# Attention kernel: one scan for a block's first piece, value rows added 1024 wide, and the operands of projection A made while the last gate runs

## The chip, the cores and the metric

The kernel runs on one core of one Trainium2 chip. Its engines work in parallel, each in the order of its own queue: PE (TensorE, matrix products; the profile lists its weight loads apart, as PEld), DVE (VectorE), ACT (ScalarE), POOL (GpSimd) and SP, which issues the DMAs. The metric is the time of one execution in microseconds of the device, lower is better. Before the change the median of three runs is 1477.73 us (1476.61 to 1478.14).

## The reference, cut to what matters

One layer of an encoder: 1024 positions, width 1024. Branch A is softmax attention over a band of nine chunks with a learned bias, branch B is stick-breaking attention; each has 8 heads of 64. The branches are projected, gated, added, projected once more, and followed by a norm, a gated feed-forward and a second norm.

```python
h = x @ w_in
y_a = chunk_band_attention(qa, ka, va, rel_bias) @ w_proj_a
y_b = stick_breaking_attention(qb, kb, vb) @ w_proj_b
mix = (sigmoid(ga + b_a) * y_a + sigmoid(gb + b_b) * y_b) @ w_out
x = layer_norm(alpha * x + mix)
x = layer_norm(alpha * x + (silu(g) * u) @ w_ffn_out)      # g, u = split(x @ w_ffn_in)

# branch B, for every query t and key s < t:
#   weight[t, s] = sigmoid(z[t, s]) * product over s < j < t of sigmoid(-z[t, j])
```

## The kernel before, in words

All products are in fp32 made of three passes of rounded operands: `split` (lines 106 and 107) rounds a tile on ACT and subtracts on DVE, so a tile `x` becomes `xh` and `xl`. The stages, by the profiled execution's clock: projections of the input (to 289 us), attention (289 to 688), projection B and output projection (688 to 860), feed-forward in (860 to 1259) and feed-forward out (1259 to the end).

In attention the 16 heads (8 of A, then 8 of B) run one behind the other. The rows of the sequence are reversed, so key positions run forward from the diagonal. A head has eight query blocks of 128; the first four make row group g = 0 and the last four g = 1. For a block, PE computes scores into a PSUM bank (`sc`, two banks). In A (`soft_block`) DVE adds the bias and takes the running minimum (line 494, listed as ISA in the order of instructions), ACT takes the exponential (499), DVE a reciprocal (501), POOL multiplies (502). In B (`stick_block`) ACT makes sigmoid(-z) in `kp` and sigmoid(z) in `be`; DVE turns `kp` into running products by scans along the row; POOL multiplies `be` by them (537). A block of B wider than 512 is cut into two pieces. Its first 128 columns hold the diagonal: there the scan multiplies and adds the identity, which starts the product at 1; further on nothing is to be added. `ident_ps` is a PSUM bank that holds the identity in its first 128 columns and zeros behind.

`value_steps` then transposes weights on PE (558, tile `tp`), splits them (tile `pt`), and multiplies by the values into one PSUM bank (`pv`, 571 and 572), two steps behind the transposes. At the end of a row group ACT copies `pv` out (578), and DVE adds its lower 64 rows to its upper 64 rows (579). Two heads make one tile `yt` of 128x1024, which is stored to `y_dr` (581); the last tile, number 7, stays in SBUF.

Between these steps PE is filled with the units of `fill_all`: first gates 4 to 15 (48 matmuls each, line 420), then projection A (608), whose operands `yh` and `yl` come from `y_dr` through `reload_y` (load on SP, rounding on ACT at 632, subtraction on POOL at 633). `yh` and `yl` take the buffers (tag `xt`) that hold the gates' operand. A scheduler in the framework sets the order of each engine's queue from the written order and its own model of times, and buffers come in rings (`SLOTS`), so an edit in one place can move rows elsewhere.

After attention, projection B works on tiles c = 6, 7, 5, 4, 0, 1, 2, 3, two halves each: 12 matmuls into a `sc` bank, then on DVE a product with the gate `gB` (736), a sum with A's part (737) and a subtraction (107), with ACT's rounding `mh` between. SP loads `gB`, and the output weights `wr_o` into a ring of three buffers; each `wr_o` is rounded on ACT (403) and subtracted on DVE (404, `wl_o`).

Of the kernel before, what the change touches and what calls it, by code (L numbers as in the profile page):

```python
# [14 lines left out]
ALU = mybir.AluOpType  # L15
# [3 lines left out]
P = 128  # L19
# [3 lines left out]
DH = 64  # L23
# [10 lines left out]
LO, HI = slice(0, HW), slice(HW, 2 * HW)  # L34
# [14 lines left out]
def hybrid_trunk_kernel(ctx: ExitStack, tc, x, xt, w_in, b_gate, rel_bias, w_proj,  # L49
# [6 lines left out]
    nc = tc.nc  # L56
# [7 lines left out]
    def slot(tag, name, dtype=F32):  # L64
        return pool.tile([P, 1024], dtype, tag=tag, name=name, bufs=SLOTS[tag])
# [10 lines left out]
    def bank(tag, name):  # L76
        return ps.tile([P, HW], F32, tag=tag, name=name, bufs=BANKS[tag])

    def dram(name, n):
        return [dr.tile([P, 1024], F32, name=f"{name}{i}") for i in range(n)]  # L80
# [3 lines left out]
    dma = nc.sync.dma_start  # L84
# [12 lines left out]
    y_dr = dram("y_dr", 8)  # L97
# [7 lines left out]
    def split(dst_h, dst_l, src):  # L105
        nc.scalar.copy(dst_h, src)  # L106
        nc.vector.tensor_tensor(dst_l, src, dst_h.bitcast(F32), ALU.subtract)  # L107
# [302 lines left out]
    def load_gate(i, lo_eng):  # L410
        return load_w(w_in[24 + (i % 2) * 8 + i // 2], f"g{i}", of("op"), of("op"), lo_eng)

    def gate(i, w):
        gt = slot("gt", f"gate{i}")
        for hf, cs in enumerate((LO, HI)):
            acc = bank("mm", f"gps{i}_{hf}")
            for k in range(KT):
                ks = slice(k * P, (k + 1) * P)
                for j, (lw, rx) in enumerate(((w[0], xh), (w[0], xl), (w[1], xh))):
                    mm(acc, lw[:, ks], rx[k][:, cs], start=(k == j == 0),  # L420
                       stop=(k == KT - 1 and j == 2))
                    yield 1.0
            nc.scalar.copy(gt[:, cs], acc)
        dma(g_dr[i], gt)
# [34 lines left out]
    def scores(name, hd, b, c0, n):  # L459
        q = hd["qs"][:, b * P:(b + 1) * P]  # L460
        ksl = slice(b * P + c0, b * P + c0 + n)
        sc = bank("sc", name)
        mm(sc[:, 0:n], q, hd["kh"][:, ksl], start=True, stop=False)
        mm(sc[:, 0:n], q, hd["kl"][:, ksl], start=False, stop=True)  # L464
        return sc
# [40 lines left out]
    def ident_ps():  # L506


        if not aside:
            aside.append(bank("tr", "ident_ps"))  # L510
            nc.vector.memset(aside[0], 0.0)
            nc.vector.tensor_copy(aside[0][:, 0:P], ident)
        return aside[0]

    def stick_block(hd, b, be):

        nm = f"b{hd['n']}_{b}"
        w = (8 - b) * P
        kp = slot("kp", f"kp_{nm}")
        nc.gpsimd.memset(be[:, 0:1], 0.0)  # L520
        c1 = max((4 - b) * P, 320)
        cuts = [(0, c1), (c1, w - c1)] if b < 4 else [(0, w)]
        for c0, n in cuts:
            sc = scores(f"sc_{nm}_{c0}", hd, b, c0, n)
            e = c0 + n
            m0 = max(c0, 1)
            nc.scalar.activation(kp[:, c0:e], sc[:, 0:n], AF.Sigmoid, scale=-1.0)  # L527
            nc.scalar.activation(be[:, m0:e], sc[:, m0 - c0:n], AF.Sigmoid)
            if c0 == 0:

                nc.vector.tensor_tensor_scan(kp[:, 0:P], kp[:, 0:P], ident_ps()[:, 0:P], 0.0,
                                             ALU.mult, ALU.add)
            s0 = max(c0, P)
            if s0 < e:
                nc.vector.tensor_tensor_scan(kp[:, s0:e], kp[:, s0:e], ident_ps()[:, 0:e - s0],  # L535
                                             kp[:, s0 - 1:s0], ALU.mult, ALU.bypass)
            nc.gpsimd.tensor_tensor(be[:, m0:e], be[:, m0:e], kp[:, m0 - 1:e - 1], ALU.mult)  # L537

    def value_steps(hd, g, wt):

        br, h = hd["br"], hd["h"]
        reach = (4, 8)[br]
        q0 = 4 * g
        nm = f"{'ab'[br]}{hd['n']}_{g}"
        pv = []

        kbs = [4, 5, 6, 7, 3, 2, 1, 0] if g == 0 else [7, 6, 5, 4]
        steps = []
        for i, kb in enumerate(kbs):
            lo_q = max(q0, kb - reach)  # L550
            hi_q = min(q0 + 3, kb)
            n = (hi_q - lo_q + 1) * P
            pts = []

            def turn(kb=kb, lo_q=lo_q, hi_q=hi_q, n=n, pts=pts):
                tp = bank("tr", f"tp_{nm}_{kb}")
                for qb in range(lo_q, hi_q + 1):
                    tr(tp[:, (qb - lo_q) * P:(qb - lo_q + 1) * P],  # L558
                       wt[qb - q0][:, (kb - qb) * P:(kb - qb + 1) * P], ident)
                pt = slot("pt", f"pt_{nm}_{kb}", F32R)  # L560
                split(pt[:, 0:n], pt[:, HW:HW + n], tp[:, 0:n])
                pts.append(pt)

            def mult(i=i, kb=kb, lo_q=lo_q, n=n, pts=pts):
                v = hd["v"]
                if i == 0:
                    pv.append(bank("pv", f"pv_{nm}"))
                last = i == len(kbs) - 1
                cs = slice((lo_q - q0) * P, (lo_q - q0) * P + n)
                pt = pts[0]  # L570
                mm(pv[0][:, cs], v[:, kb, :], pt[:, 0:n], start=(i == 0), stop=False)
                mm(pv[0][:, cs], v[:, kb, :], pt[:, HW:HW + n], start=False, stop=last)
                if last:
                    yt = hd["yt"]()
                    r = slice(h * DH, (h + 1) * DH)
                    gs = slice(g * HW, (g + 1) * HW)
                    both, cs = (yt, gs) if h == 0 else (slot("yt", f"yv_{nm}"), LO)
                    nc.scalar.copy(both[:, cs], pv[0])
                    nc.vector.tensor_tensor(yt[r, gs], both[0:DH, cs], both[DH:P, cs], ALU.add)
                    if h == 1 and g == 1 and hd["i"] < 7:  # L580
                        dma(y_dr[hd["i"]], yt)

            steps.append((turn, mult, i == 0))
        return steps


    def fill_all():
        w = first_w
        for i in range(first_gate, 16):
            nxt = load_gate(i + 1, nc.gpsimd) if i < 15 else load_proj(0, 0, "op", nc.gpsimd)  # L590
            yield from gate(i, w)
            w = nxt
        for i in range(4):
            reload_y(i, nc.gpsimd)
        for cc in range(4):
            nxt = load_proj(0, cc + 1, "op", nc.gpsimd) if cc < 3 else None
            if cc < 3:
                reload_y(4 + cc, nc.gpsimd)
            for j in range(2):
                c = 2 * cc + j  # L600
                t = slot("gt", f"gA{c}")
                reload_gate(t, c, 0)
                for hf, cs in enumerate((LO, HI)):
                    acc = bank("mm", f"yAps{c}_{hf}")
                    for k in range(4):
                        ks = slice(j * HW + k * P, j * HW + (k + 1) * P)
                        for n, (lw, rx) in enumerate(((w[0], yh), (w[0], yl), (w[1], yh))):
                            mm(acc, lw[:, ks], rx[k][:, cs], start=(k == n == 0),  # L608
                               stop=(k == 3 and n == 2))
                            yield 1.0  # L610
                    nc.vector.tensor_tensor(t[:, cs], acc, t[:, cs], ALU.mult)
                if c < KEEP:
                    dma(m_dr[c], t)
                else:
                    kept[c] = t
            w = nxt

    def load_proj(br, cc, raw, eng):

        return load_w([(cs, w_proj[2 * cc + j][:, br * HW:(br + 1) * HW])  # L620
                       for j, cs in enumerate((LO, HI))], f"y{br}_{cc}", of(raw), of("op"), eng)
# [2 lines left out]
    KEEP, kept = 5, {}  # L624
    yh, yl = [None] * 8, [None] * 8

    def reload_y(i, eng):
        raw = slot("op", f"yraw{i}")
        dma(raw, y_dr[i])
        yh[i] = slot("xt", f"yh{i}", F32R)  # L630
        yl[i] = slot("xt", f"yl{i}", F32R)
        nc.scalar.copy(yh[i], raw)
        eng.tensor_tensor(yl[i], raw, yh[i].bitcast(F32), ALU.subtract)

    def reload_gate(t, c, br):
        dma(t, g_dr[2 * c + br])
        col = br * 8 + c
        nc.scalar.activation(t, t, AF.Sigmoid, bias=bg[:, col:col + 1])

    fill = fill_all()  # L640
    state = dict(t=0.0, done=False)

# [78 lines left out]
    for n, c in enumerate((6, 7, 5, 4, 0, 1, 2, 3)):  # L721
        if n % 2 == 0:
            w = load_proj(1, c // 2, "op", nc.vector)
# [359 lines left out]
```

## Time and profile before

| | |
|---|---|
| median of the runs | 1477.73 us |
| the profiled execution's own time | 1479.15 us |
| its span in the trace | 1477.4 us |
| TensorE clock granted, mean | 0.996 |
| DVE busy in the span | 994.8 us |
| 24 added halves of value rows, L579 on `yt` and `yv_b` | 16.5 + 8.3 us |
| 8 more, on `yv_a` | 6.2 us |
| scans of B, L531 and L535 | 26.6 + 78.5 us |

A row of the grouped view reads: line, engine, operation, out<-in, shapes, count, then total busy time, mean ns of one, and the idle time of the engine just before, with what ended it. A row of the timeline reads: start, duration, engine, line, operation, out<-in, shape, count, and in brackets the engine's idle time before it and what it waited for.

### The profile page before, as it was taken

Reading aid. Unit: us, or ns where it says so; the run is one execution under the profiler, and the core shown is the slowest. Engines: PE = TensorE matmul, PEld = TensorE weight load, DVE = VectorE, ACT = ScalarE, POOL = GpSimd, SP = SyncE. Lnnn points to the kernel's source line nnn. Section 1 sums busy time; section 2 is a strip of 40 time slices with the busy share of each in tenths; the row PEclk is TensorE's granted clock in tenths of the full one; section 3 lists DMA queues with packets and bytes.
Section 4 is the critical chain, followed back from the end, with each engine's and each line's share of the span. In section 5 each row is a group of like instructions: output and inputs, shape, how many; then the busy total and the mean of one; then the engine's idle time right before and its main releaser. Section 6 shows DMA issues by size and latency. Waiting matters only on the chain.

```text
span 1477.4 us, 19005 instructions
## 1 busy us (share of the span) xinstructions
PE 1433.8 (97%) x6728; PEld 1177.4 (80%) x6728; DVE 994.8 (67%) x1633; ACT 679.5 (46%) x1215; POOL 314.5 (21%) x333
## 2 busy tenths in 40 slices
PE   8999999999998999999999899999999999999997
PEld 6788888887787888777788678888888888888886
DVE  8865555276677767786848985555555543885896
ACT  6444444376676656874513443333333332344540
POOL 0000000143336555960003212111111111300021
PEclk9999999999999999999999999999999999999999
DMA  6555544766554355657611133323233335863521
GB/s 214 157 186 171 162 149 158 217 194 175 157 152 135 92 163 188 200 186 242 243 43 58 58 111 125 100 100 105 102 107 103 105 107 207 313 228 93 182 83 72
DMA packets 76176, 219.42 MB, mean 149 GB/s; under 512 B 9504, under 2 KB 9504, under 8 KB 76080
## 3 DMA queue, kind: packets, MB, share of 16 engines
q1 hardware_dynamic: 76080, 218.19, 45.6%
q8 instruction: 53, 0.87, 0.2%
q14 instruction: 43, 0.35, 0.1%
HBM read 149.71 MB, written 68.45 MB: 148 GB/s over the span
## 4 chain that ended last, share of the span: by engine, by line
PE 77%; DVE 9%; DMA 5%; ACT 3%; issue 2%; POOL 2%; SPq 0%; POOLq 0%; DVEq 0%; ACTq 0%
PE sxf L173 15%; PE dn L970 14%; PE sxp L173 9%; PE szf L173 7%; PE gps L420 5%; PE szp L173 5%; PE syf L173 4%; PE syp L173 2%; DVE kp_b L535 2%; PE ops L116 2%; PE ops L114 2%; PE ops L113 2%; PE tp_b L558 2%; PE yAps L608 1%; PE tp_a L558 1%
## 5 line engine op out<-in xcount | busy, mean ns | idle before, releaser
L970 PE MATMUL dn<-dr,dl 128*128 128x512 f32 x924 | 209.6, 389 | 0.0
L970 PEld LDWEIGHTS dn<-dr,dl 128*128 128x128 f32 x924 | 173.4, 188 | 36.1
L537 POOL TENSOR_TENSOR w_b<-w_b,kp_b 128x511 f32<-128x511 f32 (+3 forms) x96 | 99.1, 1036 | 62.2 <-DVE kp_b L535 34.5
L752 POOL TENSOR_TENSOR mv<-mv,neghalf 128x1 f32<-128x1 f32 x16 | 26.9, 1682 | 315.4 <-DVE mv L751 311.4
L106 ACT CAST dl<-raw 128x512 fp32r<-128x512 f32 x77 | 47.5, 623 | 84.8 <-PE dn L970 67.9
L535 DVE TENSOR_TENSOR_SCAN kp_b<-kp_b,ident_ps 128x384 f32<-128x384 f32 (+6 forms) x88 | 78.5, 892 | 4.6
L420 PE MATMUL gps<-xh,wl_g 128*128 128x512 f32 x192 | 80.3, 418 | 0.0
L420 PE MATMUL gps<-xh,wh_g 128*128 128x512 f32 x192 | 80.3, 418 | 0.0
L420 PE MATMUL gps<-xl,wh_g 128*128 128x512 f32 x192 | 80.2, 418 | 0.0
L107 DVE TENSOR_TENSOR dl<-raw,dl 128x512 fp32r<-128x512 f32 x77 | 53.5, 701 | 25.1 <-ACT dl L106 24.7
L527 ACT ACTIVATE kp_b<-sc_b 128x512 f32<-128x512 f32 (+3 forms) x96 | 48.3, 504 | 41.1 <-PE sc_b L464 31.0
L502 POOL TENSOR_SCALAR w_a<-w_a,st_a 128x640 f32<-128x640 f32 (+2 forms) x64 | 46.1, 724 | 82.7 <-DVE st_a L501 69.9
L107 DVE TENSOR_TENSOR pt_b<-tp_b,pt_b 128x512 fp32r<-128x512 f32 (+1 forms) x96 | 51.1, 542 | 18.3 <-ACT pt_b L106 18.2
L481 POOL MEMSET bias<- 64x64 f32 x8 | 1.2, 145 | 275.9 <-ACT bias L480 275.9
L827 POOL TENSOR_TENSOR sb<-h 128x512 f32<-128x512 f32 x10 | 17.8, 1778 | 193.0 <-PE syf L173 97.4
L173 PE MATMUL szf<-x1S63h,wcf 128*128 128x512 f32 x176 | 57.7, 389 | 0.0
L106 ACT CAST pt_b<-tp_b 128x512 fp32r<-128x512 f32 (+1 forms) x96 | 47.8, 498 | 20.8 <-PE tp_b L558 20.3
L106 ACT CAST pt_a<-tp_a 128x512 fp32r<-128x512 f32 (+1 forms) x96 | 40.3, 424 | 27.2 <-PE tp_a L558 26.7
L499 ACT ACTIVATE w_a<-w_a,st_a 128x640 f32<-128x640 f32 (+2 forms) x64 | 44.6, 697 | 17.4 <-DVE st_a L494 16.6
L558 PE MATMUL tp_b<-ident,w_b 128*128 128x128 f32 x288 | 48.3, 275 | 4.2 <-DVE pt_b L107 1.8
L186 DVE TENSOR_TENSOR gt<-sxf,gt 128x512 f32<-128x512 f32 x22 | 15.1, 688 | 54.6 <-PE sxf L173 54.6
L107 DVE TENSOR_TENSOR pt_a<-tp_a,pt_a 128x512 fp32r<-128x512 f32 (+1 forms) x96 | 45.6, 485 | 8.2 <-ACT pt_a L106 8.1
(1541 smaller groups left out, 4218.9 us busy)
## 6 DMA issues: line engine op xcount, KB each, us to landing
raw<-left_dr SPq DMA_DIRECT2D x77, 256.0 KB, 3.0
wLf<-in_w_ffn_in_dram SPq DMA_DIRECT2D x22, 512.0 KB, 3.9
wRf<-in_w_ffn_in_dram SPq DMA_DIRECT2D x22, 512.0 KB, 4.2
rows<-in_w_ffn_out_dram SPq DMA_DIRECT2D x22, 512.0 KB, 6.1
left_dr<-h SPq DMA_DIRECT2D x33, 256.0 KB, 2.0
v_dr<-v SPq DMA_DIRECT2D x16, 512.0 KB, 3.6
kl<-k_dr SPq DMA_DIRECT2D x32, 256.0 KB, 6.4
v<-v_dr SPq DMA_DIRECT2D x16, 512.0 KB, 3.3
```

The lines of the kernel that those rows point to most:

```text
L106: nc.scalar.copy(dst_h, src)
L107: nc.vector.tensor_tensor(dst_l, src, dst_h.bitcast(F32), ALU.subtract)
L113: mm(acc, lh, rh, start=(i == 0), stop=False)
L173: mm(acc, lw[:, ks], rx, start=(first and kt == i == 0), stop=(kt == 3 and i == 2), skip_group_check=not first)
L420: mm(acc, lw[:, ks], rx[k][:, cs], start=(k == j == 0), stop=(k == KT - 1 and j == 2))
L499: nc.scalar.activation(s[:, 0:w], s[:, 0:w], AF.Exp, bias=st[:, m:m + 1], scale=-1.0, accum_out=st[:, 2:3])
L502: nc.gpsimd.tensor_scalar(s[:, 0:w], s[:, 0:w], st[:, 3:4], 0.0, ALU.mult, ALU.add)
L527: nc.scalar.activation(kp[:, c0:e], sc[:, 0:n], AF.Sigmoid, scale=-1.0)
L535: nc.vector.tensor_tensor_scan(kp[:, s0:e], kp[:, s0:e], ident_ps()[:, 0:e - s0], kp[:, s0 - 1:s0], ALU.mult, ALU.bypass)
L537: nc.gpsimd.tensor_tensor(be[:, m0:e], be[:, m0:e], kp[:, m0 - 1:e - 1], ALU.mult)
L558: tr(tp[:, (qb - lo_q) * P:(qb - lo_q + 1) * P], wt[qb - q0][:, (kb - qb) * P:(kb - qb + 1) * P], ident)
L970: mm(acc, lw, rx, start=(fresh and steps[s][1] == n == 0), stop=(last and n == 2), skip_group_check=not fresh)
```

## The change

Three edits. **Scans:** a piece of a block of B is scanned whole. The first piece starts from 0.0 and adds `ident_ps` over its full width, the second continues by multiplication alone, as before. **Value rows:** the second head of a pair keeps one tile `yv` for both row groups, and the halves are added once for both groups, 64x1024 wide, after the second; for tile 7 they are still added by row group. **Operands:** `reload_y` becomes `load_y` and `split_y`; for tiles 0 to 3 both are called between the units of gate 15, where they stood behind it.

```diff
-            if c0 == 0:
-                nc.vector.tensor_tensor_scan(kp[:, 0:P], kp[:, 0:P], ident_ps()[:, 0:P], 0.0,
-                                             ALU.mult, ALU.add)
-            s0 = max(c0, P)
-            if s0 < e:
-                nc.vector.tensor_tensor_scan(kp[:, s0:e], kp[:, s0:e], ident_ps()[:, 0:e - s0],
-                                             kp[:, s0 - 1:s0], ALU.mult, ALU.bypass)
+            nc.vector.tensor_tensor_scan(kp[:, c0:e], kp[:, c0:e], ident_ps()[:, 0:n],
+                                         kp[:, c0 - 1:c0] if c0 else 0.0,
+                                         ALU.mult, ALU.bypass if c0 else ALU.add)
...
-                    both, cs = (yt, gs) if h == 0 else (slot("yt", f"yv_{nm}"), LO)
-                    nc.scalar.copy(both[:, cs], pv[0])
-                    nc.vector.tensor_tensor(yt[r, gs], both[0:DH, cs], both[DH:P, cs], ALU.add)
+                    if h == 1 and "yv" not in hd:
+                        hd["yv"] = slot("yt", f"yv_{nm}")
+                    both = hd.get("yv", yt)
+                    nc.scalar.copy(both[:, gs], pv[0])
+                    if hd["i"] == 7:
+                        nc.vector.tensor_tensor(yt[r, gs], both[0:DH, gs], both[DH:P, gs], ALU.add)
+                    elif g == 1:
+                        nc.vector.tensor_tensor(yt[r], both[0:DH], both[DH:P], ALU.add)
...
-            yield from gate(i, w)
+            for n, unit in enumerate(gate(i, w)):
+                if i == 15:
+                    if n in (6, 12, 18, 26):
+                        load_y((6, 12, 18, 26).index(n))
+                    if n in (28, 34, 40, 46):
+                        split_y((28, 34, 40, 46).index(n), nc.gpsimd)
+                yield unit
             w = nxt
-        for i in range(4):
-            reload_y(i, nc.gpsimd)
...
-                reload_y(4 + cc, nc.gpsimd)
+                load_y(4 + cc)
+                split_y(4 + cc, nc.gpsimd)
...
+    def load_y(i):
+        yraw[i] = slot("op", f"yraw{i}")
+        dma(yraw[i], y_dr[i])
+
+    def split_y(i, eng):
+        raw = yraw.pop(i)
         yh[i] = slot("xt", f"yh{i}", F32R)
         yl[i] = slot("xt", f"yl{i}", F32R)
```

On DVE in the third head of A, at the end of its first row group (the rows of block 3, `sc_a_3`, and the transposed weights `pt_a`). Before:

```order
L107 TENSOR_TENSOR pt_a_1_6_2872<-tp_a_1_6_2868,pt_a_1_6_2872 128x384
L579 TENSOR_TENSOR yt_2625<-yv_a_0_2878 64x512
L494 ISA w_a_0_3_2788,st_a_3_2882<-sc_a_3_0_2883,bias_2697 128x320
L501 RECIPROCAL st_a_2_2856<-st_a_2_2856 128x1
L107 TENSOR_TENSOR pt_a_1_5_2897<-tp_a_1_5_2894,pt_a_1_5_2897 128x256
L494 ISA w_a_0_3_2788,st_a_3_2882<-sc_a_3_1_2887,bias_2697,st_a_3_2882 128x320
L494 ISA w_a_1_0_2906,st_a_4_2908<-sc_a_4_0_2909,bias_2697 128x512
L501 RECIPROCAL st_a_3_2882<-st_a_3_2882 128x1
```

The same place now:

```order
L107 TENSOR_TENSOR pt_a_1_6_2871<-tp_a_1_6_2867,pt_a_1_6_2871 128x384
L494 ISA w_a_0_3_2787,st_a_3_2880<-sc_a_3_0_2881,bias_2696 128x320
L494 ISA w_a_0_3_2787,st_a_3_2880<-sc_a_3_1_2885,bias_2696,st_a_3_2880 128x320
L501 RECIPROCAL st_a_2_2855<-st_a_2_2855 128x1
L107 TENSOR_TENSOR pt_a_1_5_2895<-tp_a_1_5_2892,pt_a_1_5_2895 128x256
L494 ISA w_a_1_0_2904,st_a_4_2906<-sc_a_4_0_2907,bias_2696 128x512
L501 RECIPROCAL st_a_3_2880<-st_a_3_2880 128x1
```

The addition is gone from this place (it stands, 1024 wide, eight computing rows further on, behind `pt_a_0_5`), and both passes over block 3 now stand ahead of the reciprocal of block 2.

On DVE in the fourth head of B, around its blocks 2 to 4. Before:

```order
L531 SCALAR_TENSOR_TENSOR kp_b_2_5634<-kp_b_2_5634,ident_ps 128x128
L535 SCALAR_TENSOR_TENSOR kp_b_2_5634<-kp_b_2_5634,ident_ps 128x192
L535 SCALAR_TENSOR_TENSOR kp_b_2_5634<-kp_b_2_5634,ident_ps 128x448
L107 TENSOR_TENSOR pt_b_1_6_5655<-tp_b_1_6_5651,pt_b_1_6_5655 128x384
L579 TENSOR_TENSOR yt_5337<-yv_b_0_5663 64x512
L531 SCALAR_TENSOR_TENSOR kp_b_3_5668<-kp_b_3_5668,ident_ps 128x128
L535 SCALAR_TENSOR_TENSOR kp_b_3_5668<-kp_b_3_5668,ident_ps 128x192
L535 SCALAR_TENSOR_TENSOR kp_b_3_5668<-kp_b_3_5668,ident_ps 128x320
L107 TENSOR_TENSOR pt_b_1_5_5688<-tp_b_1_5_5685,pt_b_1_5_5688 128x256
```

And now:

```order
L529 SCALAR_TENSOR_TENSOR kp_b_2_5588<-kp_b_2_5588,ident_ps 128x320
L529 SCALAR_TENSOR_TENSOR kp_b_2_5588<-kp_b_2_5588,ident_ps 128x448
L107 TENSOR_TENSOR pt_b_1_6_5608<-tp_b_1_6_5604,pt_b_1_6_5608 128x384
L529 SCALAR_TENSOR_TENSOR kp_b_3_5620<-kp_b_3_5620,ident_ps 128x320 x2
L107 TENSOR_TENSOR pt_b_1_5_5639<-tp_b_1_5_5636,pt_b_1_5_5639 128x256
```

Each block's first two scans became one, and the addition between blocks 2 and 3 is gone.

On ACT in projection B (`wh_o`, `wh_y` are weights being rounded, `mh` the rounded sums, `gB` a gate). Before:

```order
L403 CAST wh_o_0_7373<-wr_o_0_7372 128x1024
L106 CAST mh_7010<-mA_7154 128x512
L403 CAST wh_o_1_7379<-wr_o_1_7378 128x1024
L403 CAST wh_y_1_7276<-wr_y_1_7275 128x1024
L638 ACTIVATE gB_7282<-gB_7282,bg 128x1024
L403 CAST wh_o_2_7385<-wr_o_2_7384 128x1024
```

And now:

```order
L403 CAST wh_o_1_7301<-wr_o_1_7300 128x1024
L106 CAST mh_6932<-mA_7076 128x512
L403 CAST wh_o_2_7307<-wr_o_2_7306 128x1024
L403 CAST wh_y_1_7198<-wr_y_1_7197 128x1024
L648 ACTIVATE gB_7204<-gB_7204,bg 128x1024
L403 CAST wh_o_3_7313<-wr_o_3_7312 128x1024
```

Every `wh_o` stands one place earlier against the gates and sums (`wh_o_0` three rows ahead of this piece). DVE's `wl_o` rows moved with them, and on SP the loads of `wr_o_2` and of the second half's `wr_o_1` now stand ahead of a `gB` load each, where they stood behind it. The four subtractions `yl` of tiles 0 to 3 on POOL and the four roundings `yh` on ACT stand at the same rows of their queues in both kernels; of their loads on SP, the third and fourth moved some five rows up, ahead of the loads of a head's `qs` and `kl`.

More of the change, by code (lines that the diff above doesn't have):

```diff
@@ L625, in hybrid_trunk_kernel @@
     yh, yl = [None] * 8, [None] * 8
-    def reload_y(i, eng):
-        raw = slot("op", f"yraw{i}")
-        dma(raw, y_dr[i])
+    yraw = {}
+    def load_y(i):
[3 more added lines that the diff above has]
+        raw = yraw.pop(i)
         yh[i] = slot("xt", f"yh{i}", F32R)
```

## The prediction

> **What bounds the kernel now.** I read the shares of busy time first, then the same by stage, then the waits of PE and of its weight loads within attention.
>
> ```profile
> PE 1433.8 (97%) x6728; PEld 1177.4 (80%) x6728; DVE 994.8 (67%) x1633; ACT 679.5 (46%) x1215; POOL 314.5 (21%) x333
> ```
> ```profile
> 289.00:453.00 164.00, 155.39 (x890) 128.53 (x888) 117.20 (x381) 114.45 (x281) 69.18 (x98) 1.00 0.56 161
> 453.00:688.00 235.00, 227.58 (x1198) 187.84 (x1198) 172.13 (x274) 156.87 (x332) 131.82 (x160) 1.00 0.54 169
> ```
>
> PE is the bound of the whole. The two stages that the change touches are attention A and B; the columns are start and end, length, then busy time of PE, PEld, DVE, ACT and POOL. PE idles 164.00 − 155.39 = 8.6 us in A and 7.4 us in B, 16.0 together, and DVE is busy for 71% and 73%. So no work saved on DVE counts by itself: all that the change can win in attention lies in those 16.0 us, and only where DVE or ACT stands ahead of the engine that ended a wait.
>
> ```profile
> PE yAps L608 <- POOL yl L633: 2.6, 2, 1.4
> PE tp_a L558 <- POOL w_a L502: 2.5, 7, 0.8
> PE pv_a L571 <- ACT yt L578: 1.9, 1, 1.9
> PE tp_b L558 <- DVE pt_b L107: 1.8, 6, 0.5
> ...
> PE tp_a L558 <- DVE pt_a L107: 1.3, 2, 0.9
> PE tp_b L558 <- POOL w_b L537: 1.1, 1, 1.1
> PE tp_b L558 <- DVE pt_a L107: 1.0, 1, 1.0
> ```
> ```profile
> PEld tp_a L558 <- POOL w_a L502: 5.3, 8, 1.2
> PEld tp_b L558 <- POOL w_b L537: 4.4, 7, 1.3
> PEld pv_a L571 <- ACT yt L578: 4.2, 5, 2.3
> PEld yAps L608 <- POOL yl L633: 3.5, 2, 1.8
> ```
>
> These are the waits of the stretch from 289 to 690 us: total, times, longest. A matmul's recorded end is modelled, so PE's own idle time understates a wait, and that of the weight loads (PEld), which run ahead, overstates it. I take the middle of the two where both list it.
>
> **The change, part by part.** First what it does to DVE.
>
> ```profile
> L531 DVE TENSOR_TENSOR_SCAN kp_b<-kp_b,ident_ps 128x128 f32<-128x128 f32 x64 | 26.6, 416 | 30.1 <-ACT kp_b L527 27.6 <-ACT w_b L528 2.0
> L535 DVE TENSOR_TENSOR_SCAN kp_b<-kp_b,ident_ps 128x512 f32<-128x512 f32 x16 | 20.5, 1279 | 1.5
> ...
> L535 DVE TENSOR_TENSOR_SCAN kp_b<-kp_b,ident_ps 128x384 f32<-128x384 f32 x16 | 16.2, 1014 | 0.5
> ```
> ```profile
> L107 DVE TENSOR_TENSOR yl<-yt,yh 128x1024 fp32r<-128x1024 f32 x1 | 1.2, 1226 | 1.1 <-ACT yh L106 1.1
> ```
> ```profile
> 368.65 0.69 DVE L579 TENSOR_TENSOR yt<-yv_a 64x512 f32<-64x512 f32 x1
> ```
>
> Scans: 128 more columns cost 1279 − 1014 = 265 ns, 2.07 ns each, so 416 ns for the first 128 hold some 150 that don't grow. A first piece of 512 in one scan is then 150 + 512 × 2.07 = 1.21 us, where it was 416 + 1014 ns = 1.43: 0.215 us less. Seven blocks of each of 8 heads lose a scan: 56 × 0.215 = 12.0 us of DVE. Unknown is the rate of the adding form beyond 128 columns. If nothing of its 416 ns were fixed (3.25 ns each), 512 take 1.66 us, 0.23 more than now; if it ran like a plain addition, (1226 − 690) / 512 = 1.05 ns each, 416 + 384 × 1.05 = 0.82, which is 0.61 less. I take the row of the continuing scans, since it is the nearest operation. [...]
>
> Value rows: 28 additions of 0.69 become 14 of about 1.23 (a plain subtraction of that width): 28 × 0.69 − 14 × 1.23 = 2.1 us of DVE. Tile 7 keeps its four. The 14 us in all are hidden beside PE except at these places.
>
> **a) Head ends in A.**
>
> ```profile
> 370.80 0.69 DVE L494 CUSTOM_DVE_ANT_0 w_a<-sc_a,bias 128x512 f32<-128x512 f32 x1
> ```
> ```profile
> 373.16 0.33 PE L558 MATMUL tp_a<-ident,w_a 128*128 128x128 f32 x1 [0.29 <-POOL w_a L502]
> ```
>
> The transposes of block 3 wait for POOL's product, and POOL for DVE's reciprocal. The addition at 368.65 stood ahead of that reciprocal, so 0.69 leaves the chain. But the order shows the reciprocal now behind the pass over block 4 (370.80, 0.69 as well), both passes of block 3 start earlier, and in five heads PE asks for this transpose 0.47 us sooner, ahead of two value matmuls and one of a gate. The wait is 2.5 by PE and 5.3 by PEld; its first instance (0.8 and 1.2) is ahead of any removed addition and stays: 1.7 to 4.1, middle 2.9. I take −1.2, as the gain is certain for ACT's exponential and doubtful for the reciprocal; bounds 0 to −2.9.
>
> **b) Copying out in A.**
>
> ```profile
> 374.63 0.62 ACT L499 ACTIVATE w_a<-w_a,st_a 128x384 f32<-128x384 f32 x1
> ```
> ```profile
> 375.24 0.58 ACT L578 COPY yv_a<-pv_a 128x512 f32<-128x512 f32 x1
> ```
>
> The next value matmuls need the bank that this copy empties. In five heads ACT's order has the copy ahead of this exponential, so the bank comes free 0.62 sooner. PEld's waits there but the longest are about 0.5 each (4.2 − 2.3 over 4), and the middle between PE (which lists none of the short ones) and PEld gives 4 × 0.25 = 1.0; of the longest (1.9 on PE, 2.3 on PEld) at most 0.6 can go, and I take 0.4. −1.4; bounds 0 to −2.5, all of the short ones on PEld and the 0.6.
>
> **c) From A to B.**
>
> ```profile
> 450.12 1.36 DVE L579 TENSOR_TENSOR yt<-yv_a 64x512 f32<-64x512 f32 x1
> ```
> ```profile
> 450.89 2.81 POOL L404 TENSOR_TENSOR wl_g<-wr_g,wh_g 128x1024 fp32r<-128x1024 f32 x1
> ```
> ```profile
> 454.61 0.33 PE L558 MATMUL tp_b<-ident,w_b 128*128 128x128 f32 x1 [1.05 <-POOL w_b L537]
> ```
>
> Here DVE is behind, and PE waits three times from 450 to 455: the smaller of two for `pt_a` in the list above (1.3 − 0.9 = 0.4), and the single ones of 1.0 and 1.1. The addition of 1.36 moves behind them, and four merged scans save 0.86, so DVE comes 2.2 us earlier. But POOL, in order, is held by `wl_g` until 453.7, and its products end the last wait. So the two waits on DVE go mostly, the third stays: −1.0; bounds 0 to −2.5, all three.
>
> **d) Rows of B.**
>
> ```profile
> 564.83 1.48 DVE L579 TENSOR_TENSOR yt<-yv_b 64x512 f32<-64x512 f32 x1
> ```
> ```profile
> 567.55 1.85 POOL L537 TENSOR_TENSOR w_b<-w_b,kp_b 128x319 f32<-128x319 f32 x2 [1.79 <-DVE kp_b L535]
> ```
> ```profile
> 568.86 0.63 PE L558 MATMUL tp_b<-ident,w_b 128*128 128x128 f32 x4 [0.55 <-DVE pt_b L107]
> ```
>
> This is the chain that the change shortens best: the addition (1.48), then the scans of the next block, then POOL, which had waited 1.79 for them, then PE. Gone are the whole addition at the middle of a head and 0.2 per block. The class is 1.8 by PE for `pt_b` (six times) and 4.4 − 1.3 = 3.1 by PEld for `w_b` without the instance of c. PE's waits of half a microsecond are shorter than what leaves the chain, so most of them should go, and between 1.8 and 3.1 I take 2.2, nearer to PE's own row. −2.2; bounds −0.5 to −3.1, the former if the scans that add take 0.23 more and only the addition is gained.
>
> **e) Tile 6.**
>
> ```profile
> 635.84 0.69 DVE L579 TENSOR_TENSOR yt<-yv_b 64x512 f32<-64x512 f32 x1 [0.52 <-ACT yv_b L578]
> ```
> ```profile
> 644.62 1.05 ACT L632 CAST yh<-yraw 128x1024 fp32r<-128x1024 f32 x1 [1.34 <-DMA yraw<-y_dr]
> ```
>
> The last addition of a pair is now 1.23 where it was 0.69, 0.54 later. For tile 6 the store to `y_dr` and the reload follow at once, and ACT already stands 1.34 waiting for it, with copies and casts of B behind. +0.5; bounds 0 to +0.6.
>
> **f) Projection B**, which no edit names, but whose queues moved.
>
> ```profile
> 706.14 6.09 SPq L402 DMA_DIRECT2D wr_o<-in_w_out_dram  x3
> 712.51 0.33 SPq L636 DMA_DIRECT2D gB<-g_dr  x1
> ```
> ```profile
> 711.66 1.04 ACT L403 CAST wh_o<-wr_o 128x1024 fp32r<-128x1024 f32 x1
> 719.68 1.16 ACT L638 ACTIVATE gB<-gB,bg 128x1024 f32<-128x1024 f32 x1 [2.65 <-DMA gB<-g_dr]
> ```
> ```profile
> 723.33 0.50 PE L113 MATMUL yBps<-yh,wh_y 128*128 128x512 f32 x1 [1.23 <-DVE gB L736]
> ```
>
> Tile 3's gate load went out at 712.51 and came 7.1 us later, at 719.6; ACT stood 2.65 us for it, with the rounding of `mh` behind, and DVE and PE (723.33) behind that. Now this load is queued on SP behind the second half's `wr_o_1`, which needs the buffer of `wr_o_2`, that is, the end of `wl_o_2`. Loaded from 706.14 in about 5.4 us (the cast at 711.66 could start), rounded in 1.04 and subtracted in 1.22, `wl_o_2` ends at 713.9; with two issues of 0.33 the gate goes out at 714.3, and 1.8 us later than now comes all that hangs on it. DVE has gained 1.2 us there by a `wl_o` that now stands earlier, but waits for ACT at this point anyway. +1.8. Bounds: −1.2, if the load is early enough and that `wl_o` counts; +3.4, if the weight takes 7.1 us as the gate did.
>
> **Sum:** −1.2 − 1.4 − 1.0 − 2.2 + 0.5 + 1.8 = −3.5 against the profiled execution, 1479.15 us. It stands 1.42 above the median of the runs, 1477.73. So 1475.65 for a profiled execution, and 1474.2 for a median.
>
> **The rivals.** *The gains are hidden* (R1): each of a to d shortens one of two or three chains that end close together. In a the reciprocal is behind one pass more, in c POOL is in order; for it speaks that PE already waits only 0.3 to 0.6 at a time; against it, that in d POOL itself waits 1.79 for DVE. Half of a to d then: −2.9 + 0.5 + 1.8 = −0.6, which is 1477.1.
>
> *Wide additions collide with POOL* (R2).
>
> ```profile
> 601.55 4.70 POOL L633 TENSOR_TENSOR yl<-yraw,yh 128x1024 fp32r<-128x1024 f32 x2
> ```
> ```profile
> 604.71 2.08 DVE L579 TENSOR_TENSOR yt<-yt 64x512 f32<-64x512 f32 x1 [1.01 <-ACT yt L578]
> ```
>
> An addition of two SBUF operands took 2.08 beside POOL's `yl`, 0.69 alone. If twice the width meets POOL as the rows at 450.12 and 564.83 did, it takes some 2.9 instead of 1.23 in B, 1.7 more at the end of each head, ahead of the next one's scans; d then falls to its lower bound and b by 0.4: +2.1, so 1476.3. [...]
>
> *The third edit does what its words say* (R3): `yl` would be there when the projection asks, and the waits on it, 2.6 by PE and 3.5 by PEld, go: 3.1 more, 1471.1. Against it stands the order: the four `yl` and `yh` stand at the rows where they stood, since their buffers hold the gates' operand until the last gate has read it. Only two loads come earlier, and POOL's 4.70 at 601.55 are POOL's own work. That this edit does nothing is my forecast.
>
> *Slower* (R4): the gate load behind the weight ring in f. With weight and gate each taking d us, the gate lands at 708.8 + 2d instead of 719.6, so each microsecond counts twice, and ACT blocks for it. The loss is 2d − 10.8; it eats the 5.3 of the other terms from d = 8.0 on. The longest there was 7.1, so it needs more load on the DMA queues. At 9.5 it is 8.2, the sum +2.9, and the time 1480.6.
>
> **How the numbers follow.** Forecast 0.48, R1 0.24, R2 0.10, R3 0.10, R4 0.08. The forecast's own range is 1471 to 1477, from its bounds taken not all at once. 0.2% is 3.0 us, about what a measurement of this kernel can tell from no change: faster means under 1474.8. The forecast is that in somewhat under two cases of three (0.31), R3 nearly always (0.10), R1 and R2 rarely (0.04): 0.45. Slower, over 1480.7, is half of R4 and the tail of R1 with f at its upper end: 0.10. The same: 0.45. The range, 1469.5 to 1479.5, takes in R1 to R3 and leaves out R4 and the ends.
>
> **What would show it.** Scans of 512 at 1.21 us, 64x1024 additions at 1.2 to 1.3 (2.9 would be R2), DVE at about 981 us busy. a to d: PE busy unchanged, with idle time in 289 to 688 of about 10.2 instead of 16.0; the waits on `pt_b` and on ACT's copy gone or halved, that on `w_a` down by a third. e: ACT's wait for `yraw` at 1.9. f: ACT's wait for the last `gB` at 4 to 5 and PE's after it at about 3. R3: no wait of `yAps` on `yl`. I would be wrong above all if PE's idle time moves from one row of the list to another, or if the gate's load is not late.

## The result, and the profile after

The changed kernel takes 1472.71 us (median of 19 runs, 1470.44 to 1479.38), the kernel before beside it 1478.14 (19 runs, 1474.62 to 1480.81). The ratio is 0.9967, 95% interval 0.9957 to 0.9976: 4.9 us less, by the interval 3.5 to 6.4.

The profiled execution of the changed kernel was its slowest, 1479.38 us, 6.7 above the median, so a second one was taken with the same kernel (`e1_after_again`, 1472.21 us). Its busy times, and the two stretches shown of before:

```profile
PE 1430.2 (97%) x6728; PEld 1177.3 (80%) x6728; DVE 978.7 (67%) x1563; ACT 679.8 (46%) x1215; POOL 309.6 (21%) x333
```
```profile
289.00:453.00 164.00, 156.58 (x904) 130.29 (x902) 115.50 (x371) 115.94 (x283) 70.95 (x102) 1.00 0.57 163
453.00:688.00 235.00, 229.66 (x1214) 191.81 (x1213) 163.94 (x221) 157.03 (x333) 127.72 (x156) 1.00 0.57 182
```

DVE has 16 us less to do, and PE idles 7.4 and 5.3 us in these stretches, 12.7 together, where it was 8.6 and 7.4, 16.0 together. PE's waits from 289 to 690 us, in the same execution (total, times, longest):

```profile
PE tp_a L553 <- POOL w_a L502: 1.7, 7, 0.5
PE pv_a L566 <- ACT yt L575: 1.4, 1, 1.4
PE tp_b L553 <- DVE pt_b L107: 1.4, 1, 1.4
PE yAps L613 <- DMA g_dr<-gate: 1.4, 1, 1.4
PE tp_b L553 <- POOL w_b L520: 1.3, 1, 1.3
PE sc_b L463 <- ACT w_b L528: 1.0, 2, 0.6
PE yAps L613 <- POOL yl L643: 0.9, 1, 0.9
PE tp_a L553 <- DVE pt_a L107: 0.5, 2, 0.4
```

The six small waits of `tp_b` on `pt_b` (1.8) are gone, and one of 1.4 has come. The two of `yAps` are still there: the one put down to a DMA follows the `yl` before it, as PEld's list has both under `yl` (3.1, 2 times).

To see where the time goes, I matched PE's instructions one by one and took the start in this execution less the start in the first profile of before (us):

| clock of before | 285 | 430 | 460 | 590 | 640 | 690 | 740 | 840 | end |
|---|---|---|---|---|---|---|---|---|---|
| start now less before | −0.5 | −2.4 | −3.6 | −6.0 | −8.2 | −7.5 | −8.1 | −8.1 | −7.3 |

So 1.9 come in A, 1.2 at the change to B, 4.6 in B up to 640, 0.7 is given back, and 0.6 comes in projection B. The 0.5 ahead of attention and the 0.8 given back behind 840 us lie where no edit is. Before's profile was 1.0 above the median beside it (1478.14) and this one 0.5 below its own, so these 7.3 are more than the 5.4 between the medians. Two executions of one kernel differ by such amounts too: the second profile of before, taken later, starts these instructions up to 1.9 us earlier or 0.7 later than the first.

The scans and additions of the same execution, by shape:

```profile
L529 DVE TENSOR_TENSOR_SCAN kp_b<-kp_b,ident_ps 128x512 f32<-128x512 f32 x32 | 40.0, 1249 | 14.4 <-ACT kp_b L527 12.8
L579 DVE TENSOR_TENSOR yt<-yt 64x1024 f32<-64x1024 f32 x7 | 12.6, 1795 | 1.6 <-ACT yt L575 1.4
L579 DVE TENSOR_TENSOR yt<-yv_a 64x1024 f32<-64x1024 f32 x4 | 4.9, 1222 | 1.4 <-ACT yv_a L575 1.4
```

Half of the 32 scans are second pieces as before (1279 ns); for a mean of 1249 the merged ones take 1219, where I had 1.21 us. A wide addition takes 1222 ns alone, where I had 1.23 us.

### The profile page after: what moved, and what is told of

Its sections match the earlier page's. It is cut to its first block, busy times and chain, and to the rows that moved or that the text cites. A ratio compares the mean times of both kernels' runs of the same rounds, so it can differ in the third digit from the quotient of the medians.

```text
span 1477.6 us, 18938 instructions
## 1 busy us (share of the span) xinstructions
PE 1435.4 (97%) x6728; PEld 1181.5 (80%) x6728; DVE 983.7 (67%) x1563; ACT 680.1 (46%) x1215; POOL 309.3 (21%) x333
## 4 chain that ended last, share of the span: by engine, by line
PE 81%; DVE 8%; DMA 4%; ACT 3%; issue 2%; POOL 2%; SPq 0%; POOLq 0%; DVEq 0%; ACTq 0%
PE sxf L173 15%; PE dn L980 14%; PE sxp L173 9%; PE szf L173 7%; PE gps L420 7%; PE szp L173 5%; PE syf L173 4%; PE yAps L613 2%; PE syp L173 2%; PE tp_b L553 2%; PE ops L116 2%; PE ops L114 2%; PE ops L113 2%; PE tp_a L553 1%; DVE w_a L494 1%
## 5 line engine op out<-in xcount | busy, mean ns | idle before, releaser
L529 DVE TENSOR_TENSOR_SCAN kp_b<-kp_b,ident_ps 128x512 f32<-128x512 f32 (+3 forms) x96 | 93.1, 970 | 44.2 <-ACT kp_b L527 40.9
L116 PE MATMUL ops<-wh_o,ml 128*128 128x512 f32 x128 | 50.2, 392 | 0.2 <-DVE ml L107 0.2
```

Of the source, the lines that this page charges most:

```text
L116: mm(acc, ll, rh, start=False, stop=(i == n))
L529: nc.vector.tensor_tensor_scan(kp[:, c0:e], kp[:, c0:e], ident_ps()[:, 0:n], kp[:, c0 - 1:c0] if c0 else 0.0, ALU.mult, ALU.bypass if c0 e ...
```

## The experiments

Theory D is the prediction's: DVE comes earlier at the row starts of B, by both edits on it. Q and W are its rivals on the shares of the edits; P is on the long addition that the first profile showed. C and L, on PE's waits for `yl`, came up with these profiles.

**The change again, and its edits one by one.** The three kernels of one edit each are the kernel before with the lines of that edit from the diff above.

```diff
# e1_scans
+            nc.vector.tensor_tensor_scan(kp[:, c0:e], kp[:, c0:e], ident_ps()[:, 0:n],
+                                         kp[:, c0 - 1:c0] if c0 else 0.0, ...
# e1_rows
+                    elif g == 1:
+                        nc.vector.tensor_tensor(yt[r], both[0:DH], both[DH:P], ALU.add)
# e1_operands
+                    if n in (6, 12, 18, 26):
+                        load_y((6, 12, 18, 26).index(n))
+                    if n in (28, 34, 40, 46):
+                        split_y((28, 34, 40, 46).index(n), nc.gpsimd)
```

> The changed kernel once more, since its profiled execution (1479.38 us) lies 6.7 us above the median of its runs (1472.71). Theory D (DVE comes earlier at the row starts of B): ratio 0.9967 again, 4.5 to 5.5 us under before, and in a profile of about 1473 us the 64x1024 addition that took 8.25 us beside POOL, and the wait of 2.3 us of PE behind it, are there too, since nothing in their order changes from run to run. Rival P (that addition is blocked only in some executions, and these are the slow ones): the addition takes under 3 us here and the wait is gone.

> Only the first edit, the merged scans. Theory D: 12 us of DVE go, of which 1.5 to 2.5 us reach the end (the waits of PE at 511, 528, 540 and 568 us shrink, none vanishes). Rival Q (the gain is the wide additions' and what they move): 0 to 0.5 us. Rival W (the wide additions cost what they save beside POOL): 4 to 5 us, all of the change's gain or more.

> Only the second edit, the value rows added 1024 wide; projection B's queues move with it as in the whole change. Theory D: 2 to 3 us less. Rival Q: 4 to 5 us less. Rival W: no gain, 0 to 1 us more. In the projection of B my prediction had 1.8 us lost; the changed kernel's profile shows 1.1 gained from 690 to 725 us, so this one should gain it too.

> Only the third edit, projection A's operands called for between the units of gate 15. All of theory D, Q and W: within 0.5 us of before, with both waits of yAps on yl (1.3 and 1.4 us of PE) still there. A rival by which two earlier loads matter: 1 us or more less, with one of these waits gone.

| kernel | ratio to before | 95% interval | median, us |
|---|---|---|---|
| e1_after_again | 0.9960 | 0.9944 to 0.9975 | 1473.71 |
| e1_scans | 0.9985 | 0.9973 to 0.9997 | 1476.49 |
| e1_rows | 0.9974 | 0.9961 to 0.9988 | 1473.69 |
| e1_operands | 1.0001 | 0.9990 to 1.0013 | 1479.00 |

By the ratios, the scans bring 2.2 us, the value rows 3.8, the third edit nothing; 6.0 together, which agrees with the whole (4.9 and 5.9). Theory D and rival Q differ less here than the intervals are wide (1.8 us and more to each side): the scans lie where D had them, the rows between the two. Rival W fell. The third edit left both waits on `yl` as they were.

On the long addition theory D was wrong and rival P right. It is the same instruction in the two executions of one kernel, first the one of 1479.38 us with POOL's row behind it, then the second:

```profile
598.19 8.25 DVE L579 TENSOR_TENSOR yt<-yt 64x1024 f32<-64x1024 f32 x1 [1.26 <-ACT yt L575]
599.65 2.41 POOL L404 TENSOR_TENSOR wl_y<-wr_y,wh_y 128x1024 fp32r<-128x1024 f32 x1
601.98 1.04 POOL L532 TENSOR_TENSOR w_b<-w_b,kp_b 128x383 f32<-128x383 f32 x1
602.93 2.42 POOL L643 TENSOR_TENSOR yl<-yraw,yh 128x1024 fp32r<-128x1024 f32 x1
```
```profile
597.96 2.62 DVE L579 TENSOR_TENSOR yt<-yt 64x1024 f32<-64x1024 f32 x1 [1.26 <-ACT yt L575]
599.46 3.39 POOL L404 TENSOR_TENSOR wl_y<-wr_y,wh_y 128x1024 fp32r<-128x1024 f32 x1
```

In the second, the addition lies across the border of two of POOL's instructions (599.49), and POOL's `wl_y` behind it takes 3.39 for 2.41: 0.98 more, about what DVE needs for the addition alone (1.22). In the first, POOL goes through three more instructions, to 605.35, each within 0.03 of its mean in that profile (2.40, 1.01 and 2.41), and DVE's addition ends at 606.44. Both times the addition ends 1.09 us behind the end of one of POOL's instructions. I read these rows as one engine standing while the other's instruction runs. Why DVE stood for three more of POOL's instructions in one execution and for none in the other, no run shows. PE then waited 2.3 us for `pt_b`, queued on DVE behind the addition. By the starts of PE's instructions the first execution loses 5.3 us from 600 to 620 us; that wait is one part of it, and a lower clock, shown next, the other.

**The clock behind the two waits, and who pays for B's wide additions.**

```diff
# e2_before_again: the kernel before, unchanged
# e2_wide_a (from the changed kernel)
-                    if hd["i"] == 7:
+                    if hd["i"] >= 4:
# e2_y_dve4, and e2_y_dve2 with DVE for n = 34 and 46 only (from the changed kernel)
-                        split_y((28, 34, 40, 46).index(n), nc.gpsimd)
+                        split_y((28, 34, 40, 46).index(n), nc.vector)
```

> The kernel before once more, for a second profile. In two profiles so far (the changed kernel's first, and the merged scans alone) the granted TensorE clock fell to 0.50 to 0.73 for about 4 us right after PE's two waits on yl, at 600 to 612 us, and 5.1 and 2.5 us were lost there; in three others it stayed at 1.00. Theory C (PE's own waits of 1.3 and 1.4 us close together let the clock drop, in some executions of every kernel that has these waits): it can be seen here too, whatever the time. Rival: it belongs to the changed kernels alone. Second question: in projection B (690 to 725 us) all four later profiles come 0.6 to 1.0 us closer than this kernel's first profile, with or without moved queues, so this one should gain as much, and the moved queues are worth nothing.

> The changed kernel, but the value rows of B (tiles 4 to 7) added by row group, 64x512 wide, as before; those of A stay 1024 wide. Theory D: the addition at the middle of each head of B is back at the row starts; with the scans merged about half of what was gained there (4.6 us from 460 to 650 us by the second profile) goes: 2 to 3 us over the changed kernel. Rival P (the wide additions of B pay for themselves beside POOL: 8.25 us once, 2.6 at other times): no loss, or 1 us less than the changed kernel.

> The changed kernel, with the four subtractions yl of tiles 0 to 3 on DVE (1.22 us each alone) instead of POOL (2.4 us each, three almost in a row). Theory C: PE's two waits on yl (0.9 to 1.4 us each) go, 2 to 2.5 us, and with them the drops of the clock at 600 us, some 1 us more in the median, so 3 us less than the changed kernel. Rival L (DVE with two operands in SBUF is kept out as long as POOL has an instruction running, as in the addition of 8.25 us): the waits on yl stay or grow, now on DVE, and the scans behind them come late: 0 to 4 us more.

> The changed kernel, with the subtractions yl of tiles 1 and 3 on DVE and those of tiles 0 and 2 on POOL. Theory C: both waits shrink to under 0.5 us each, 2 us less than the changed kernel. Rival L: DVE's two are held behind POOL's and gain nothing: within 1 us of the changed kernel.

| kernel | ratio to before | 95% interval | median, us |
|---|---|---|---|
| e2_before_again | 0.9996 | 0.9985 to 1.0007 | 1477.07 |
| e2_wide_a | 0.9968 | 0.9957 to 0.9979 | 1473.09 |
| e2_y_dve4 | 0.9940 | 0.9926 to 0.9953 | 1469.21 |
| e2_y_dve2 | 0.9954 | 0.9939 to 0.9969 | 1470.61 |

The stretches behind PE's two waits, start and end, length, busy times of five engines, then the granted clock (third number from the end): first the changed kernel's first profiled execution, then its second.

```profile
600.00:604.00 4.00, 4.00 (x14) 3.40 (x14) 4.00 (x1) 2.28 (x4) 4.00 (x3) 0.57 0.33 128
```
```profile
600.00:604.00 4.00, 4.00 (x26) 3.48 (x25) 3.46 (x6) 3.15 (x8) 4.00 (x3) 1.00 0.28 106
```

PE is busy in both, but at 0.57 of the clock it has 14 matmuls in the stretch instead of 26. The kernel before shows it too, in its second profile; and with the `yl` on DVE:

```profile
604.00:608.00 4.00, 2.64 (x12) 2.33 (x12) 2.48 (x2) 2.05 (x5) 4.00 (x2) 0.76 0.65 199
```
```profile
600.00:604.00 4.00, 4.00 (x24) 3.39 (x23) 3.29 (x7) 1.76 (x4) 4.00 (x5) 1.00 0.87 285
```

Of the eight profiles whose PE waits twice for `yl` (0.9 to 1.4 us each within 3 us), four show such a drop; of the six where at most one of the waits is left, none. So theory C holds for the place, and the drop is no mark of the change. Nor was PE idle for long there: in the changed kernel's first profile its two waits by the matmuls' starts were 1.1 and 1.5 us, with matmuls between; and in its second they were 0.9 and 1.4 by the list, and the clock stayed at 1.00.

The traces' own clock records say more than the stretches of 4 us. In each of the 14 profiles all drops start a whole number of steps of 3.413 us apart. In the changed kernel's first profile they start at 600.27, 607.10, 846.03 and 1474.08 us, the last three 2, 72 and 256 steps behind the first, and the clock is at 0.50 for 1, 1 and 3 steps and then to the end. These steps are what I call the grid of an execution. In attention (290 to 690 us) the eight steps with the least busy time of PE (0.33 to 0.48 of the step, by the records) are each followed by a drop, and of the other steps at full clock (0.49 and up) none is. The two profiles of the changed kernel differ in this way:

| profile | step of its grid, us | PE busy | clock in the next step |
|---|---|---|---|
| first | 596.86 to 600.27 | 1.45 of 3.41 | 0.50 |
| second | 595.31 to 598.72 | 1.99 of 3.41 | 1.00 |
| second | 598.72 to 602.13 | 2.58 of 3.41 | 1.00 |

Both have the same two waits on `yl`, but in the first they fall almost whole into one step, and in the second the border of two steps, at 598.72 us, lies within the second wait (598.2 to 599.55). The second drop of the first profile, at 607.1 us, follows the step with PE's wait of 2.3 us behind the long addition (busy for 0.33 of it). Outside attention one step does not fit: 0.45 at 843.2 us of before's first profile, with no drop right behind it.

`e2_y_dve4` beats both kernels: 0.9940, 3 to 4 us less than the changed one (0.9967 and 0.9960), and its five runs lie within 2.0 us. Rival L fell. `e2_y_dve2` lies between, with one wait of 1.1 us left. `e2_wide_a` is at 0.9968, as the whole change: beside merged scans the additions of B cost the same narrow or wide, and theory D's 2 to 3 us were wrong. By the starts of PE's instructions, this kernel comes 2.0 us forward from 460 to 590 us with the additions of B narrow, `e1_scans` 1.5 with all of them narrow, `e1_rows` 2.2 with the scans unmerged, and the whole change 2.4: either edit alone takes away most of those waits.

**The edits without the waits on `yl`.**

```diff
# e3_before_y (from the kernel before)
-            reload_y(i, nc.gpsimd)
+            reload_y(i, nc.vector)
# e3_y_rows: e2_y_dve4 with the scans of before
# e3_y_scans: e2_y_dve4 with the value rows of before
# e3_y_dve7 (from e2_y_dve4)
-                split_y(4 + cc, nc.gpsimd)
+                split_y(4 + cc, nc.vector)
```

> The kernel before, with only the four subtractions yl of tiles 0 to 3 on DVE. Theory C: the two waits on yl (2.6 us by PE) and the drops of the clock behind them go, 3 to 4 us less than before, the runs lie within 3 us of each other (6 us without), and the clock stays at 1.00 from 596 to 616 us. Rival: the gain of 3.5 us that this brought on top of the change needs the room that the change made on DVE; here 0 to 1.5 us.

> The yl on DVE and the second and third edit, with the scans of before: together with the next run and the one above, the change's two edits one by one without the noise of the clock's drops. If the edits add up as singly measured before (3.8 us for the value rows, 2.2 for the scans): 3.5 to 4 us less than the run above. If the rows count in A alone, where their waits were: 2 us less.

> The yl on DVE, the scans merged and the third edit, with the value rows of before. If scans count at the row starts of B alone: 1.5 to 2.5 us less than the first of this group; and about 0.7 given back by the new wait of 1.4 us of PE at 650 to 660, which is in all profiles with merged scans (0.5 and 0.3 in the others).

> The changed kernel with all seven yl that are reloaded on DVE. The later three (tiles 4 to 6) are not in PE's list of waits: within 0.7 us of the kernel with four on DVE (ratio 0.9940). If DVE is by now late at the row starts of B's last heads, 1 us more.

| kernel | ratio to before | 95% interval | median, us |
|---|---|---|---|
| e3_before_y | 0.9998 | 0.9986 to 1.0009 | 1477.81 |
| e3_y_rows | 0.9945 | 0.9932 to 0.9958 | 1470.24 |
| e3_y_scans | 0.9961 | 0.9948 to 0.9974 | 1472.59 |
| e3_y_dve7 | 0.9952 | 0.9937 to 0.9966 | 1471.92 |

Here theory C failed and its rival was right: on the kernel before, the same move gains nothing. The waits on `yl` did go, and the clock stayed at 1.00, but PE waits elsewhere. Its list from 590 to 622 us, and DVE's load there:

```profile
PE tp_b L558 <- POOL w_b L537: 1.1, 1, 1.1
PE sc_b L463 <- ACT w_b L528: 0.9, 1, 0.9
PE tp_b L558 <- DVE pt_b L107: 0.4, 1, 0.4
```
```profile
600.00:604.00 4.00, 4.00 (x26) 3.45 (x24) 3.96 (x6) 4.00 (x7) 3.46 (x3) 1.00 0.33 92
604.00:608.00 4.00, 3.81 (x19) 2.77 (x18) 3.96 (x4) 4.00 (x8) 4.00 (x3) 1.00 0.41 119
```

These 2.4 us stand where the two waits on `yl` (2.6) stood before: DVE is full (3.96 of 4.00) and its scans now come late instead of the `yl`. This profile also has 1.3 us more of waiting at 366 to 369 us in A (`sc_a` on `st_a`, 1.9 for 0.6), which is not the edit's: up to 590 us every engine's order is that of before. There ACT waited 2.7 us for the load of a gate's weight (`wr_g`), as it did in the profile of `e3_y_scans` (2.6) and in none of the other twelve. With either of the two edits, DVE has room: 0.9945 with the rows, 0.9961 with the scans, 7.8 and 5.5 us under `e3_before_y`, both more than expected; both together (`e2_y_dve4`) 8.6. So each of them alone opens most of it, and here they don't add. The spread of the runs, which theory C had under 3 us, was 7.1 in `e3_before_y`. Whether drops of the clock cause it is not shown: the profiled run has none in attention, but of its twelve runs the four with the lowest mean clock (0.993 and 0.994) take 1477.88 to 1482.22 us, and the other eight (0.995 to 0.997) 1475.13 to 1479.04. Moving the other three `yl` as well brought nothing: 0.9952, which overlaps 0.9940 and is 1.8 us more, so neither of its two expectations is settled.

## Why the prediction came out as it did

Faster was forecast, 1474.2, and 1472.71 measured: 3.5 less against 5.4 by the two medians. The mechanism held; one term of the sum had a cost that isn't there, and another was too small.

- **What bounds it.** Right: 16 us of DVE's work went, and about a third of that came through, mostly in the waits named. The third edit does nothing, as the order had it (1.0001). R3 fell with it. The sign given for it failed: PE's busy time was not unchanged (1433.8 to 1430.2), and over the same instructions (288.5 to 680.5 us now) its idle time fell by 3.8 us, to 12.2 and not to 10.2, while they come 7.0 us closer. The idle time holds only about half of what was won; the rest lies in PE's busy time, whose ends are modelled.
- **The costs on DVE.** Right to about 10 ns: 1219 ns for 1.21 us, 1222 for 1.23; the adding form of the scan runs at nearly the rate of the other, (1219 − 416) / 384 = 2.09 ns per column against 2.07.
- **a and b.** −2.6 together, measured −1.9 by the starts. PE's wait for the copy went from 1.9 to 1.4, about as taken. That on `w_a` went from 2.5 to 1.7, less than the 1.2 taken, and PEld's wait on `w_a` rose (5.3 to 5.8); that fits the reciprocal behind one more pass, which no run separates.
- **c.** −1.0, measured −1.2. The last wait, on POOL, stayed: 1.3 in the list, now put down to a MEMSET of POOL (L520).
- **d.** −2.2, measured −4.6 up to 640 us against before's first profile: the size was off by up to two. To 590 us it is 2.4: the three waits on `pt_b` in that stretch (1.1 by the list) are gone, and that of `sc_b` on ACT is shorter (1.0 to 0.6); by the starts these four make 2.1 (511, 528, 540 and 568 us). Beyond come another 2.2: five of 0.2 to 0.5 us by the starts (597, 622, 629, 630 and 636 us; 1.8 together), which I had counted in the class but not as so many, and 0.4 of the first wait on `yl`. Two of these steps, 0.46 at 528 us and 0.48 at 622, are in before's second profile too, so some 3.7 of the 4.6 are the change's. The price of it, a new wait of 1.4 at 652 us, I had not seen; it comes with the merged scans alone (1.5 and 1.6 us by the starts in all their profiles but one of 1.2, 0.5 in the others).
- **e.** ACT's wait for `yraw` was 1.9 in the first profile, as said, and 0.9 in the second: a reload's landing changes by more than the 0.54 that the addition is later. PE shows no loss.
- **f.** This is the step that failed: "Loaded from 706.14 in about 5.4 us". The first weight, `wr_o_0`, is loaded earlier as well, so `wr_o_2` could follow right behind `wr_o_1`, at 694 us (some 701.5 by the clock of before) and not at 706, and was rounded early. I had moved one load and left those ahead of it where they were. The queueing was as I said, the gate's load 0.6 us behind the end of `wl_o_2` (703.89), but that end came early, and so the load left no later than before. The loads of `wr_o_0`, of `wr_o_1` and `wr_o_2`, and of the last gate in the second profile of the changed kernel (start, duration):

```profile
686.79 0.33 SPq L402 DMA_DIRECT2D wr_o<-in_w_out_dram  x1
...
692.32 2.06 SPq L402 DMA_DIRECT2D wr_o<-in_w_out_dram  x2
...
704.52 0.33 SPq L646 DMA_DIRECT2D gB<-g_dr  x1
```

The gate's is 8.0 us earlier than 712.51, the lead that the whole stage has by then. ACT's wait for it was 3.1 where I had 4 to 5, and PE's behind it 0.7 where I had 3. And the 7.1 us that this load took in the first profile of before was one execution's: in the second it took 6.3, and that one comes 1.2 us closer from 690 to 724 us, with no queue moved. So nothing shows that the moved queues of projection B are worth anything either way. Without this term the sum would have been −5.3 and the time 1472.4. R4, which stood on the same load, has no ground.
- **R2.** The collision is there, 8.25 us and a wait of 2.3 once, but it is a matter of the execution: 1.8 us on average in the next profile, 1.2 alone, and the medians of wide and narrow additions in B don't differ (0.9968 and 0.9967).
- **R1.** Half of a to d was too little.
- **The number.** That it came out near is in part luck. Of a to d, a and b together brought 0.7 less than taken and d up to 2.4 more, and the wait at 652 us takes 0.7 back, so these errors cancel in part.

What stays open: of the eight profiles with wide additions in A none shows a drop of the clock behind PE's wait at 396 us (1.4 to 1.7 us by the starts), and two of six with narrow ones do (1.9 to 2.1). Both are the same kind of drop, one step at 0.50 behind a step in which PE is busy for 0.42 and 0.48; in the profile that comes nearest without one it is 0.49. Where the grid lies differs from execution to execution, so whether part of the gain in the medians is of that kind, one profile per kernel can't say.

## What to carry to other kernels

Where PE is bound, as here at 97% busy, and its waits are many and short, work taken off a helper engine counts where a wait ends behind it, and it counts again as room: the same move of four subtractions to DVE was worth nothing on the kernel before (0.9998) and 3 to 4 us once DVE had been eased (0.9940 against 0.9967 and 0.9960). When a queue is reordered, follow the whole run of loads ahead of the one that matters before giving it a time; and take a second profile before building a term on one transfer's duration.

## What the runs showed that was not expected

- A DVE addition with both operands in SBUF took 8.25 us for 1.22 of work while POOL's instructions ran one behind the other, to 1.09 us ahead of its end, and 2.62 in another execution of the same program.
- Two waits of PE of 1.1 to 1.5 us within 3 us were followed, in four profiles of eight, by a granted clock of 0.50. It went with how they fall on a grid of 3.41 us that differs from execution to execution: in attention each step with PE busy for 0.33 to 0.48 of it had a drop behind it, and no step at full clock with more (0.49 and up) had one.
- The scan that starts from a number and adds takes less than the one that continues from a column and only multiplies, by about the same at 128 columns (416 and 479 ns) as at 512 (1219 and 1279). Which of the two differences does it, no run separates.
